# A decoder layer on one core: the opening written as one explicit list, with c spread by rounded products and VectorE in program order

## The chip, the core and the metric

The kernel is one program on one core of a Trainium2 chip. The core has five engines that run side by side and wait for each other on semaphores: TensorE (PE in the profile; its weight loads are shown as PEld), VectorE (DVE), ScalarE (ACT), GpSimd (POOL) and SyncE (SP), which here issues nearly all transfers. Sixteen DMA engines carry these from the memory outside (HBM) into the on-chip memory.

The metric is the time of one execution in microseconds (us). The kernel before takes 1697.94 us, the median of three runs (1695.81 to 1700.74).

## What is computed

A decoder layer on x of 256 rows and 2048 columns, all in float32. Its input is modulated by a condition vector c, two mixers and a feed-forward part follow. The head of it is what matters here:

```python
mod = jax.nn.silu(c) @ w_ada[l] + b_ada[l]
sh1, sc1, g1, sh2, sc2, g2 = jnp.split(mod[:, None, :], 6, axis=-1)
h = x * (1.0 + sc1) + sh1
y = token_mixer(h, w_in[l], ...)      # proj = h @ w_in, then two mixers
x = layer_norm(DEEPNORM_ALPHA * x + g1 * y, ln1_g[l], ln1_b[l])
...
```

So no element of h is known before sums over all of c, and no product with w_in can run before a piece of h.

## The kernel before

Everything is in one function, `layer`. A float32 matrix product is made of three faster ones: each operand is split in two parts of the rounded type float32r, hi (rounded, a CAST on ScalarE) and lo (the rest, a TENSOR_TENSOR on VectorE), and hi*hi, hi*lo and lo*hi are added in PSUM. For a weight this is `split_w` (L221 the cast, L222 the difference); the products are in `ws_mm` (L308 to L310), of 128x128 by 128x256 each.

**The opening** multiplies h by 24 blocks of 256 columns of w_in (`jobs`). The 2048 rows are 16 tiles of 128, and h, kept transposed as hTh and hTl (s_86 and s_87 in listings), becomes known tile by tile. For tile k two columns of the modulation are needed, the scale and the shift. Each is a load of 1 MB of w_ada into one of four ring buffers (r) and one sum on VectorE (`ada_sum`, L241: multiply by silu(c), add up, into adac). silu(c) must stand on all 128 partitions for it: `load_c` spreads the one row by four products with a row of ones, float32, and ScalarE's Silu reads them (L136, L137) into cb. Then `prep` makes 1+scale (sc1p, L444), x*(1+scale)+shift on ScalarE (L447) and its two parts (L229, L230).

The tiles are taken in five groups of 2, 3, 3, 4 and 4 (`GROUPS`, `startup`). For each group all 24 blocks are passed through: load, split, products, and the result is copied (first group, L489, ScalarE) or added to what is there (L491, VectorE). Five of the blocks stay in PSUM through all groups instead (mm_kept). While a group runs, the modulation columns of the next are summed: `ada_goal` says how many after each block, and `ada_opening` loads three ahead. From the ninth block of the last group on, each block also ticks the background lanes, which begin with the convolution of the second mixer (`gdn_pre`).

`step` puts a pair on the list `prog`: pre (the load and the split) and post (the products and what follows). `run(3)` writes the pres three steps ahead of the posts. That is the program's order; a scheduler then settles each engine's order, except where an instruction is pinned by keep_in_program_order. SyncE issues transfers in its order, and a load waits until its buffer is free (six for raw, four for hi and for lo).

Behind the opening come ps_ba (the small products of `add_ba`), the other products with h, and in the background the mixers in lanes that a tick moves on. The second mixer ends in `gdn_turn`, which transposes its result yb (L892), scales it and splits it into ybA; products with ybA follow (L308 to L310).

## Time and profile before

| | |
|---|---|
| median of three runs | 1697.94 us |
| the profiled execution | 1696.81 us |
| its span on the core | 1694.9 us |
| mean granted TensorE clock | 0.994 |
| TensorE busy | 1646.1 us (97% of the span) |
| VectorE busy | 1236.2 us (73%) |
| ScalarE busy | 839.8 us (50%) |
| DMA, mean over the span | 244 GB/s |

The page gives busy time by engine, then the span in 40 slices of 42.4 us with busy tenths (9 is 90% or more) and the clock that was granted to TensorE. A window's row gives busy us and the number of instructions (x) by engine, then the granted clock, the share of the DMA engines and GB/s. A row of the timeline gives start, duration, engine, line, operation, what is written and read, and in brackets how long the engine idled before and on whom. A group's row gives shapes, the count, busy us and mean ns of one, and the idle time before. Neighbouring instructions of one engine overlap a little, so that a duration is some 0.08 us longer on VectorE than the distance of two starts.

### The profile page before, as it was taken

The page shows a single profiled execution, that of the slowest core. Times are in us where ns is not written, and L with a number is a line of the kernel's source. Part 1 is how long each engine was busy: PE and PEld are TensorE (multiplying, and loading weights), DVE is VectorE, ACT ScalarE, POOL GpSimd, SP SyncE. Part 2 cuts the span into 40 slices and gives each one's busy share as a digit, 9 for nine tenths or more (in the row PEclk, how much of TensorE's full clock was granted, in tenths as well). Part 3 has the DMA queues.
Part 4 walks back from the last instruction along what each step waited for, and adds up shares of the span by engine and source line. Part 5 has one row for each costly group of instructions (what it writes and reads, how often), then busy time and mean ns, then how long its engine had stood idle before and what let it go on. Part 6 is the DMA issues. An engine that isn't in the chain of part 4 may idle for free.

```text
span 1694.9 us, 28166 instructions
## 1 busy us (share of the span) xinstructions
PE 1646.1 (97%) x11077; PEld 1478.7 (87%) x11077; DVE 1236.2 (73%) x1768; ACT 839.8 (50%) x1199; POOL 34.6 (2%) x60
## 2 busy tenths in 40 slices
PE   5899999999999999999999999999999999999997
PEld 4899999789989789889988898888888888888885
DVE  6899999687985678468998786666666666555454
ACT  3544445679653754464434454444444444333341
POOL 0000000001010000000000000000000000000000
PEclk9999999999999999999999999999999999999998
DMA  9999996566875578657999477777777777766651
GB/s 370 339 362 342 362 347 217 182 189 202 265 246 173 177 230 278 200 174 266 334 366 338 139 236 234 240 230 228 222 237 231 228 227 246 238 192 191 198 191 73
DMA packets 113751, 412.72 MB, mean 244 GB/s; under 512 B 13406, under 2 KB 14446, under 8 KB 108110
## 3 DMA queue, kind: packets, MB, share of 16 engines
q1 hardware_dynamic: 110178, 400.13, 70.2%
q0 software_dynamic: 3440, 10.80, 2.4%
q8 instruction: 87, 1.43, 0.3%
q14 instruction: 46, 0.37, 0.1%
HBM read 406.59 MB, written 4.28 MB: 242 GB/s over the span
## 4 chain that ended last, share of the span: by engine, by line
PE 62%; DVE 7%; DMA 4%; ACT 3%; issue 2%; POOL 0%; DVEq 0%; ACTq 0%; POOLq 0%
PE mm L315 17%; PE mm L319 9%; PE mm L356 7%; PE mm L358 7%; PE mm L357 7%; PE mm L308 4%; PE mm L309 4%; PE mm L310 3%; DVE lo L222 3%; DMA raw<-in_w_out 1%; DVE raw_a L241 1%; ACT hi L221 1%; DMA raw<-in_w_proj_gdn 1%; PE ps L756 1%; DMA UU<-ubd 0%
## 5 line engine op out<-in xcount | busy, mean ns | idle before, releaser
L222 DVE TENSOR_TENSOR lo<-raw,hi 128x1024 fp32r<-128x1024 f32 (+2 forms) x576 | 675.5, 1178 | 365.4 <-ACT hi L221 362.6
L221 ACT CAST hi<-raw 128x1024 fp32r<-128x1024 f32 (+2 forms) x576 | 583.6, 1017 | 721.5 <-PE mm L315 196.1
L308 PE MATMUL mm<-s,hi 128*128 128x256 f32 x1232 | 349.0, 284 | 16.1 <-ACT s L229 12.0
L310 PE MATMUL mm<-s,lo 128*128 128x256 f32 x1232 | 345.2, 281 | 8.1 <-DVE lo L222 7.9
L309 PE MATMUL mm<-s,hi 128*128 128x256 f32 x1232 | 345.1, 280 | 0.0
L315 PE MATMUL mm<-s,hi 128*128 128x512 f32 x1280 | 319.6, 392 | 0.0
L315 PEld LDWEIGHTS mm<-s,hi 128*128 128x128 f32 x1280 | 228.5, 188 | 39.5
L308 PEld LDWEIGHTS mm<-s,hi 128*128 128x128 f32 x1232 | 234.1, 190 | 21.3 <-ACT s L229 13.6
L310 PEld LDWEIGHTS mm<-s,lo 128*128 128x128 f32 x1232 | 234.1, 190 | 10.0 <-DVE lo L222 9.9
L309 PEld LDWEIGHTS mm<-s,hi 128*128 128x128 f32 x1232 | 234.4, 190 | 1.8 <-issue 1.4
L319 PEld LDWEIGHTS mm<-s,lo 128*128 128x128 f32 x1280 | 169.9, 188 | 13.6
L319 PE MATMUL mm<-s,lo 128*128 128x256 f32 x1280 | 171.9, 277 | 0.0
L357 PE MATMUL mm<-lo,ach 128*128 128x512 f32 x352 | 137.0, 389 | 0.0
L356 PE MATMUL mm<-hi,ach 128*128 128x512 f32 x352 | 137.0, 389 | 0.0
L358 PE MATMUL mm<-hi,acl 128*128 128x512 f32 x352 | 136.9, 389 | 0.0
L241 DVE CUSTOM_DVE_ANT_0 r<-r,cb,cols 128x2048 f32<-128x2048 f32 x40 | 93.5, 2348 | 9.2 <-ACT cb L137 9.2
L356 PE MATMUL mm<-hi,s 128*128 128x512 f32 x192 | 78.2, 407 | 0.0
L358 PEld LDWEIGHTS mm<-hi,acl 128*128 128x128 f32 x352 | 66.1, 188 | 13.8
L356 PEld LDWEIGHTS mm<-hi,ach 128*128 128x128 f32 x352 | 66.1, 188 | 13.7
L357 PEld LDWEIGHTS mm<-lo,ach 128*128 128x128 f32 x352 | 66.1, 188 | 13.5
L358 PE MATMUL mm<-hi,s 128*128 128x512 f32 x192 | 77.0, 401 | 0.0
L357 PE MATMUL mm<-lo,s 128*128 128x512 f32 x192 | 76.1, 396 | 0.0
(314 smaller groups left out, 2260.2 us busy)
## 6 DMA issues: line engine op xcount, KB each, us to landing
raw<-in_w_ffn_in SPq DMA_DIRECT2D x176, 512.0 KB, 4.3
raw<-in_w_in SPq DMA_DIRECT2D x160, 512.0 KB, 4.6
raw_a<-in_w_ada SPq DMA_DIRECT2D x112, 512.0 KB, 4.6
raw<-in_w_ffn_out SPq DMA_DIRECT2D x88, 512.0 KB, 4.1
r<-in_w_ada SPq DMA_DIRECT2D x40, 1024.0 KB, 8.1
raw<-in_w_in SPq DMA_DIRECT2D x48, 384.0 KB, 5.6
raw<-in_w_proj_gdn SPq DMA_DIRECT2D x32, 512.0 KB, 4.6
raw<-in_w_out SPq DMA_DIRECT2D x32, 512.0 KB, 6.3
```

What stands on the lines that cost most here:

```text
L221: s_.copy(hi, raw)
L222: low = v_.tensor_tensor(lo, raw, hi.bitcast(F32), op=OP.subtract)
L241: added = v_.tensor_tensor_reduce(out=raw, in0=raw, in1=cb[:, n * part:n * part + n], scale=1.0, scalar=cols[:, col:col + 1] if first else ...
L308: t_.matmul(o, hi[:, i, c], ah, start=(first and i == 0 and t == 0), stop=False)
L309: t_.matmul(o, hi[:, i, c], al, start=False, stop=False)
L310: t_.matmul(o, lo[:, i, c], ah, start=False, stop=(last and i == kn - 1 and t == 1))
L315: t_.matmul(box[t].rearrange("p (u i) -> p u i", u=2), hi[:, i, t * P:(t + 1) * P], both[k0 + i], start=(first and i == 0), stop=False)
L319: t_.matmul(box[t][:, :S], lo[:, i, t * P:(t + 1) * P], both[k0 + i][:, 0, :], start=False, stop=(last and i == kn - 1))
L356: t_.matmul(box[h], xh, hi[:, i, :], start=start, stop=False)
L357: t_.matmul(box[h], xh, lo[:, i, :], start=False, stop=False)
L358: t_.matmul(box[h], xl, hi[:, i, :], start=False, stop=stop)
L756: t_.matmul(ps[to, n, :], lhs(n), rhs(n), start=True, stop=True)
```

## The change

It rewrites the opening and leaves the layer's arithmetic as it was but for the spread of c.

- **c** is split into hi and lo parts, one row each, and spread by eight float32r products. Idle products on a zeroed tile, whose result nobody reads, stand before (8) and behind (40).
- **The order of tiles and blocks** is one list, `make_plan`. The five kept blocks and three others take tile 0 first, four blocks in one load, then tile 1; the other 16 blocks follow in pairs with both tiles. In later groups four kept blocks go first, tile by tile, in one load each, then the others.
- **Each modulation column** has a step of its own: `after` says at which step it is loaded and summed. The first two are loaded and summed in halves. `prep` handles one tile.
- **VectorE** is wrapped (`InOrder`), so that its instructions are pinned to program order until the last group.
- The last group ticks the lanes at 12 steps instead of 16.

```diff
+class InOrder:
+        def traced(*args, **kw):
+            ins = f(*args, **kw)
+            if self.on:
+                self.tc.keep_in_program_order(ins)
...
     def load_c():
-        ones = e2("ones", [1, P])
-        v_.memset(ones, 1.0)
+        rows = [wp.tile([P, 1088], F32R, tag="lo", name="crow", bufs=4)[0:1, :] for _ in range(4)]
...
+        s_.activation(adac[:, 95:96], epsc[:, 0:1], AF.Silu)
...
+        busy(8)
+        for i in range(4):
+            split(parts[0][i], parts[1][i], cb[0:1, 512 * i:512 * i + 512])
         for i in range(4):
...
-            t_.matmul(ps, ones, cb[0:1, 512 * i:512 * i + 512], start=True, stop=True)
+            for x in range(2):
+                tc.keep_in_program_order(t_.matmul(ps, ones, parts[x][i], start=(x == 0), stop=(x == 1)))
             s_.activation(cb[:, 512 * i:512 * i + 512], ps, AF.Silu)
+        busy(40)
...
+    def prep(f, direct=False):
+        v_.tensor_scalar(sc1p[:, f:f + 1], adac[:, 16 + f:17 + f], 1.0, None, op0=OP.add)
+        hf = e2("hf", [P, S])
+        if direct:
+            s_.activation(hTh[:, f, :], x_sb[:, f, :], AF.Identity, bias=adac[:, f:f + 1], scale=sc1p[:, f:f + 1])
+            v_.tensor_scalar(hf, x_sb[:, f, :], sc1p[:, f:f + 1], adac[:, f:f + 1], op0=OP.mult, op1=OP.add)
+            v_.tensor_tensor(hTl[:, f, :], hf, hTh[:, f, :].bitcast(F32), op=OP.subtract)
+            return
+        s_.activation(hf, x_sb[:, f, :], AF.Identity, bias=adac[:, f:f + 1], scale=sc1p[:, f:f + 1])
+        s_.copy(hTh[:, f, :], hf)
+        waiting.append(lambda: v_.tensor_tensor(hTl[:, f, :], hf, hTh[:, f, :].bitcast(F32), op=OP.subtract))
...
+            if at == 8:
+                v_.on = False
+                bg["pre"].append(gdn_pre(0))
+            if at >= 8:
+                tick()
...
+    def make_plan():
+        ids = [HELD + j for j in range(KEPT)] + [HELD - 3 + j for j in range(3)]
+        add(0, 1, ids[:4], True, [False] * 4)
+        add(0, 1, ids[4:], True, [False] * 4)
+        add(1, 1, ids[:4], False, [False] * 4)
+        add(1, 1, ids[5:] + ids[4:5], False, [True] * 3 + [False])
+        for u in range((HELD - 3) // 2):
+            add(0, 2, [2 * u, 2 * u + 1], True, [True, True])
+        after = {1: [2, 3]}
+        for m, n in enumerate([5,6,8,9,10,11]):
+            after.setdefault(n, []).append(4 + m)
...
+            for k in range(k0, k0 + kn):
+                add(k, 1, list(range(HELD, HELD + 4)), False, [end and k == KT - 1] * 4)
+            for at, i in enumerate([HELD + 4] + list(range(HELD))):
+                add(k0, kn, [i], False, [i < HELD or end], at if end else None)
...
+        for n, (k0, kn, ids, post) in enumerate(plan):
+            def pre(n=n, k0=k0, kn=kn, ids=ids):
...
+                    if g == 4:
+                        v_.on = False
...
+                raw = load_w(w_in, k0, kn, c0 if len(c0) > 1 else c0[0], 256 * len(c0))
+                for m in after.get(n, []):
+                    ada_load(m)
...
+                hi, lo = split_w(raw, kn, 256 * len(c0), False, 0)
+                while waiting:
+                    waiting.pop(0)()
+                for m in after.get(n, []):
+                    ada_next(m)
+                    if m % 2 and m < 2 * KT:
+                        prep(m // 2, m == 3)
```

Three places show how the instructions move. The first is VectorE's list from the start; ISA rows are the sums of `ada_sum` and the reading of their result. Before:

```order
L131 MEMSET ones 1x128
L241 ISA r_95,adac<-r_95,cb,cols 128x2048
L241 ISA adac 128x1
L241 ISA r_95,adac<-r_95,cb,cols 128x2048
L241 ISA adac 128x1
L241 ISA r_96,adac<-r_96,cb,cols 128x2048
L241 ISA adac 128x1
L241 ISA r_97,adac<-r_97,cb,cols 128x2048
L241 ISA adac 128x1
L222 TENSOR_TENSOR lo<-raw,hi 128x512
L444 TENSOR_SCALAR sc1p<-adac 128x2
```

And in the changed kernel, where all pinned rows have the line of the wrapper (L107):

```order
L107 TENSOR_TENSOR crow<-cb,crow 1x512 x4
L107 ISA r_95,ada_half<-r_95,cb,cols 128x1024
L107 ISA ada_half 128x1
L107 ISA r_95,adac<-r_95,cb,ada_half 128x1024
L107 ISA adac 128x1
L107 ISA r_95,ada_half<-r_95,cb,cols 128x1024
L107 ISA ada_half 128x1
L107 ISA r_95,adac<-r_95,cb,ada_half 128x1024
L107 ISA adac 128x1
L107 TENSOR_SCALAR sc1p<-adac 128x1
L107 TENSOR_SCALAR hf<-x_sb,sc1p,adac 128x256
L107 TENSOR_TENSOR s_87<-hf,s_86 128x256
```

Four whole sums before the first 1+scale have become four half sums of two columns. On SyncE the loads behind them moved too: before, four columns of w_ada and one load of x stood ahead of the first w_in; now these are two columns in halves, one tile of x, two loads of w_in, and then the two columns of tile 1.

The second place is ScalarE at the turn from the first group to the second: L511 copies a finished block, L477 and L478 make a tile of h, L260 casts a weight (128x768 from the second group on, but for the kept blocks). In the changed kernel:

```order
L260 CAST hi<-raw 128x1024
L511 COPY v_93<-mm 128x512 x3
L477 ACTIVATE hf<-x_sb,adac,sc1p 128x256
L260 CAST hi<-raw 128x1024
L478 CAST s_86<-hf 128x256
L260 CAST hi<-raw 128x1024 x2
L260 CAST hi<-raw 128x768 x4
```

Before, the turn read:

```order
L489 COPY qk_98<-mm 128x512
L221 CAST hi<-raw 128x512 x2
L489 COPY qk_99<-mm 128x512
L221 CAST hi<-raw 128x512 x3
L221 CAST hi<-raw 128x768 x4
```

The Identity of the third tile of the coming group (L477) now stands ahead of the coming group's first cast; before, no tile of h was made at the turn itself.

The third place is TensorE where the products with ybA begin; tp are the transposes of yb. Before:

```order
L892 MATMUL tp<-cst,yb_6630 128x128 x8
L356 MATMUL mm<-hi,s_86 128x512
L357 MATMUL mm<-lo,s_86 128x512
L358 MATMUL mm<-hi,s_87 128x512
```

and twelve products further on in the same list:

```order
L356 MATMUL mm<-hi,s_86 128x512
L357 MATMUL mm<-lo,s_86 128x512
L358 MATMUL mm<-hi,s_87 128x512
L308 MATMUL mm<-ybA,hi 128x256
L309 MATMUL mm<-ybA,hi 128x256
L310 MATMUL mm<-ybA,lo 128x256
```

And in the changed kernel:

```order
L390 MATMUL mm<-hi,s_86 128x512
L391 MATMUL mm<-lo,s_86 128x512
L392 MATMUL mm<-hi,s_87 128x512
L987 MATMUL tp<-cst,yb_6585 128x128 x8
L342 MATMUL mm<-ybA,hi 128x256 x2
L987 MATMUL tp<-cst,yb_6585 128x128 x4
L343 MATMUL mm<-ybA,hi 128x256
```

The products that stood between the transposes and the first ybA product are now ahead of both.

## The prediction

> **What bounds the kernel now.** I read the page first, then the opening (the first 303 us) in windows, its timeline, and groups of instructions.

> ```profile
> span 1694.9 us, 28166 instructions
> PE   5899999999999999999999999999999999999997
> DVE  6899999687985678468998786666666666555454
> PEclk9999999999999999999999999999999999999998
> DMA  9999996566875578657999477777777777766651
> ```

> TensorE (PE) is full in 38 of 40 slices. What it lacks lies in the first slices, and there VectorE (DVE) and the DMA engines are full too. So the opening has three resources near their limits, and work brought forward can meet any of them.

> ```profile
> core 0: us, PE busy (x) PEld busy (x) DVE busy (x) ACT busy (x) POOL busy (x), PEclk, DMA share, GB/s
> 0.00:10.00 10.00, 7.16 (x8) 2.49 (x8) 0.24 (x3) 3.42 (x5) 0.89 (x5) 1.00 0.75 235
> 10.00:20.00 10.00, 0.00 (x0) 0.00 (x0) 9.71 (x10) 1.82 (x4) 0.00 (x0) 1.00 1.02 408
> 20.00:30.00 10.00, 8.37 (x57) 8.37 (x58) 7.51 (x12) 5.80 (x12) 0.00 (x0) 1.00 1.02 422
> 30.00:40.00 10.00, 6.65 (x38) 6.04 (x38) 9.75 (x11) 3.62 (x6) 0.00 (x0) 0.77 1.03 405
> 40.00:50.00 10.00, 9.09 (x68) 8.89 (x68) 6.43 (x10) 6.21 (x12) 0.00 (x0) 0.89 0.98 364
> 50.00:60.00 10.00, 8.49 (x67) 7.68 (x67) 8.45 (x12) 8.73 (x18) 0.00 (x0) 1.00 0.78 260
> 60.00:80.00 20.00, 18.54 (x160) 18.01 (x158) 17.92 (x30) 9.68 (x14) 0.55 (x1) 1.00 0.99 372
> 80.00:120.00 40.00, 39.31 (x341) 39.15 (x342) 39.68 (x51) 17.70 (x26) 0.00 (x0) 1.00 0.93 350
> 120.00:180.00 60.00, 58.50 (x498) 57.29 (x497) 57.99 (x70) 26.56 (x35) 0.00 (x0) 1.00 0.95 359
> 200.00:300.00 100.00, 100.00 (x885) 100.00 (x884) 97.90 (x131) 51.39 (x67) 3.12 (x5) 1.00 0.81 286
> ...
> L456 PE MATMUL ps_ba<-s,wbh x32: 276/276/276, 303.2 to 308.5; 128*32 128x256 f32 x32
> ...
> 9.66 0.60 ACT L137 ACTIVATE cb<-ps_c 128x512 f32<-128x512 f32 x1 [1.11 <-PE ps_c L136]
> 10.29 2.35 DVE L241 CUSTOM_DVE_ANT_0 r<-r,cb,cols 128x2048 f32<-128x2048 f32 x1 [9.24 <-ACT cb L137]
> 12.56 2.35 DVE L241 CUSTOM_DVE_ANT_0 r<-r,cb,cols 128x2048 f32<-128x2048 f32 x1
> 18.33 1.96 ACT L221 CAST hi<-raw 128x512 fp32r<-128x512 f32 x3 [8.08 <-DMA raw<-in_w_in]
> 20.20 1.09 ACT L447 ACTIVATE hf<-x_sb,adac,sc1p 128x256 f32<-128x256 f32 x2
> 21.64 0.80 PE L308 MATMUL mm<-s,hi 128*128 128x256 f32 x2 [12.02 <-ACT s L229]
> ```

> Undisturbed, TensorE starts 885 products in 100 us, 0.113 us each. The opening has 24 blocks x 16 tiles x 6 = 2304 products, 260.4 us. They run from 21.6 to 303.1, where ps_ba follows. So 42.7 us are lost: 21.6 before the first product and 21.1 behind it. By counts, from 21.6 to 60 only 230 products run where 340 fit (12.4 us lost); from 60 to 180 there are 999 for 1062 (7.1 us); from 200 on, none is lost. The windows' edges make up the rest.

> **Term A, the first product.** Before, four modulation columns must land and be summed; now two do, in halves. The bytes ahead of the last half are 2.37 MB (c and cols 0.14, rel_bias 0.13, 2.10 of w_ada). The rows give 2.35 MB by 10 us and 0.41 MB/us after. The first block of w_in had 4.99 MB up to its end, so its bytes were through at 16.5; ScalarE got it at 18.33, 1.9 us later. With that lag the last half is there at 11.9. A half takes 1.2 (2.27 between two whole ones, 10.29 to 12.56), so the sums end at 13.1. ScalarE's Identity of tile 0 follows after 0.2 and takes 0.6 (half of L447's 1.09 for two): 13.9.

> ```profile
> L222 DVE TENSOR_TENSOR lo<-raw,hi 128x1024 fp32r<-128x1024 f32 x49 | 59.2, 1223 | 1.9 <-ACT hi L221 1.7
> L221 ACT CAST hi<-raw 128x1024 fp32r<-128x1024 f32 x49 | 51.3, 1055 | 53.7 <-PE mm L309 34.0 <-PE mm_kept L309 11.7 <-DVE adac L241 2.7
> L222 DVE TENSOR_TENSOR lo<-raw,hi 128x768 fp32r<-128x768 f32 x48 | 44.5, 954 | 0.0
> L241 DVE CUSTOM_DVE_ANT_0 r<-r,cb,cols 128x2048 f32<-128x2048 f32 x40 | 93.5, 2348 | 9.2 <-ACT cb L137 9.2
> L491 DVE TENSOR_TENSOR kq<-kq,mm 128x512 f32<-128x512 f32 x32 | 21.7, 684 | 5.2 <-PE mm L310 5.1
> L315 PE MATMUL mm<-s,hi 128*128 128x512 f32 x1280 | 319.6, 392 | 0.0
> ```

> In ScalarE's new order the weight's cast stands behind that Identity, so its 1.06 comes on top: the **first product is at 14.9**, 6.7 us earlier. The spread of c must be done when the first half lands. The quickest whole column landed 7.4 us behind its issue, which I take for the first, issued at 1.55:

> ```profile
> DMA to landing us min/median/max: 7.4/9.6/14.0
> ```

> So it was there at 9.0 and its half, by the same rate, 1.3 earlier, at 7.7. Four one-row casts end at 4.6 (0.65 each, as L221 at 18.33, from c's landing at 2.4), the differences at 5.6, the last product (L315: 0.39) at 6.1 and the last Silu near 7.1: hidden. The price of a rounded product from one row isn't in the trace. Its bounds are nothing and that of the float32 ones; since c's last Silu stood at 9.66 with those, the upper end delays the sums by at most 2.1. I take L315's, the same width and type. The 48 idle products cost nothing while they end before 14.9: 40 of them from 6.1 take 4.5 us at 0.113, or 8.5 at the slow rate of term B; the cover is thin in the second case (14.6).

> **Term B, the first two tiles.** The eight tile-0 blocks are 48 products, 5.4 us: TensorE is through at 20.3. Tile 1 needs two further columns. Another 3.3 MB stands ahead of the second (1.2 of weights and x, 2.1 of w_ada), so it lands at 20.0; VectorE sums it by 22.3, the Identity ends at 23.0: **2.7 us** idle. Ten steps of 24 products follow, 2.72 us each: 50.2 without a wait. VectorE's list from 23.4 to the last difference of group 0 holds ten differences (1.14 each with the overlap of 0.08), five sums (2.27) and 0.8 for two tiles, 23.6 us; casts that stand behind copies of finished products in ScalarE's order hold it up by some 3 us (an estimate from 0.6 a copy, five of them late), so it is through at 50.0, and TensorE at 50.9. The first cast of group 1 stands behind the Identity of tile 4 on ScalarE, and that behind the tenth sum, which runs from 50.0 to 52.3 and is followed by Identity (0.6) and cast (1.06): that ends at 53.9, **3.0 us** idle. Without that order the cast would have been ready; this is the one place where the explicit list adds a wait, and every later cast is queued behind it.

> Idle time also cools the clock. From 30 to 50 the granted clock was 0.77 and 0.89, and in the cold stretch a product took twice as long:

> ```profile
> 36.50:41.50 5.00, 5.00 (x24) 0.50 1.05 409
> ```

> 24 in 5 us, where 44 fit: 2.3 us lost. Two waits stood ahead of it, the longest of the opening after the first product:

> ```profile
> PE mm L308 <- ACT hi L221: 3.9, 5, 2.0
> PE mm L310 <- DVE lo L222: 3.8, 5, 1.4
> ```

> Each new gap is longer than either of these but shorter than both, and stands alone; I count two thirds of one cold stretch, **1.5 us**, between none and two. [...]

> **Term C, groups 1 to 4.** The loads, sums, differences and adds are the same in number. VectorE's work in group 2 by the rows: 3 x 1.22 + 20 x 0.95 for lo, 19 x 0.68 adds, 8 x 2.35 sums, 1.7 for the three tiles, less 0.08 overlap on each of 53, 52 us; TensorE's is 432 x 0.113 = 48.8. So VectorE lags 3.2 us there, the DMA engines have 17.5 MiB to bring, which at the 372 GB/s of 60 to 80 (a share of 0.99) takes the whole of it, and group 1 (six sums) is even. Before lost 7.1. Between 3.2 and 7.1 I take **6**, near the row that was measured, since a fixed VectorE order removes no work and lets one late column hold the blocks behind it.

> Sum: 14.9 + 2.7 + 3.0 + 1.5 + 6 = 28.1 lost instead of 42.7, so the last opening product is at 288.5, **14.6 us earlier**.

> **Term D, behind the opening.** The last group ticks the background lanes 12 times instead of 16, so the mixer's work stands 24 to 48 products later on TensorE. At the first ybA product it had a lead, which it loses:

> ```profile
> 753.56 1.03 PE L892 MATMUL tp<-cst,yb 128*128 128x128 f32 x8
> 760.98 0.28 PE L308 MATMUL mm<-ybA,hi 128*128 128x256 f32 x1
> L232 ACT ACTIVATE ybA<-tp,nwc x4: 677/683/686, 754.7 to 758.9; 128x512 fp32r<-128x512 f32 x4
> L233 DVE SCALAR_TENSOR_TENSOR ybA<-tp,nwc,ybA x4: 741/744/749, 756.3 to 760.3; 128x512 fp32r<-128x512 f32 x4
> ```

> Now eight transposes (1.03), a rounding (0.68) and a difference (0.74) stand bare: **2.5 us** given back. Bounds: 0 if the first products need less, 7.4 (753.56 to 760.98) if the whole turn is bare. The bare parts add to 2.5, so I stay there.

> Net 12.1 us. The profiled execution took 1696.8 (span 1694.9 and 1.9 around it), 1.1 under the median of 1697.9. So **1684.7**.

> **Rivals.**
> 1. *VectorE never waits.* Its opening work is 66 x 1.22 + 40 x 0.95 (lo), 76 x 0.68, 40 x 2.35, 10 for the tiles and 36 convolution steps:

> ```profile
> L583 DVE SCALAR_TENSOR_TENSOR cv<-kq,cols,cv 128x254 f32<-128x254 f32 x8 | 3.9, 482 | 0.0
> ```

> Less the overlap that is 269 us. From 7.7, with 3 us of early waits and 3 for the last block, the opening ends at 282.7, 20.4 earlier, 17.9 net: 1678.9. For: 97.9 of 100 busy from 200 to 300. Against: each late column now stops the list.
> 2. *The clock cools fully at both gaps.* Two stretches of 2.7 us lost instead of 1.5 in all: 1688.6. [...]
> 3. *Given back.* In the windows above VectorE idled 24.4 us, 9.8 of them in the first ten. If the other 14.6 come again in the new list, the opening ends at 294.3, 8.8 earlier, 6.3 net: 1690.5, or up to 1695.4 if the turn before ybA is bare as a whole. For: those idles came from casts that wait for landings and free buffers, and the buffers are the same. Against: tile 0 of eight blocks gives TensorE work while they fill.
> 4. *Slower: adds in strict order.* An add reads a finished product. In a fixed order it holds up the next block's difference, which TensorE then waits for. There are 76 adds. Before, adds waited 6.2 us in all, 0.08 each, where the order could be chosen:

> ```profile
> DVE kq L491 <- PE mm L310: 5.1, 8, 1.1
> DVE v L491 <- PE mm L310: 0.9, 2, 0.6
> ```

> At 0.35 each, passed on whole, 26.6 us are added: 1711. It is slower than before from 0.17 on. Against: differences run three blocks ahead of the add, some 6 us.
> 5. *The start doesn't move TensorE*, because the landings set the pace of all of group 0: about 1697.

> **How the numbers follow.** Forecast 0.54 (1680 to 1689; 0.25 of it without cooling, 1683.2), rival 1 0.15, rival 2 0.10, rival 3 0.12, rival 4 0.05, rival 5 0.04. The range 1675 to 1694 takes in rivals 1 to 3 and the bounds of c's spread (+2.1) and of term D; it leaves rivals 4 and 5 and some tails. About 0.3% (5.1 us) is what a measurement can tell from no change: below 1692.8 lie the forecast, rivals 1 and 2 and two thirds of 3, 0.87; the rest of 3 and rival 5 make 0.08; slower 0.05.

> **What would show it.** Right: first product near 14.9 behind a cast; idle TensorE near 20 to 23 and 51 to 54; the last opening product near 288; a wait of 2 to 3 us before ybA. Wrong: a first product after 17 (landings), a halved clock between 24 and 45 (cooling), more than 10 us lost from 54 to 180 with adds waiting for products (rival 4), or more than 5 us more idle behind the opening.

## The result and the profile after

The changed kernel takes 1688.72 us, the median of 6 runs (1685.69 to 1690.71), beside 1699.09 for the kernel before. The ratio is 0.9937, with a 95% interval from 0.992 to 0.9954. The profiled execution took 1687.22 us and its span is 1685.1, 9.8 us shorter than before. The forecast had been 1684.7. So the time lies in the forecast range of 1675 to 1694, and the gain is 0.6% where 0.8% was forecast.

First the head of the page of the changed kernel: span, busy tenths, clock and DMA in 40 slices, now of 42.1 us.

```profile
span 1685.1 us, 28203 instructions
PE   8999999999999999999999999999999999999997
DVE  7899999888985687568988786666666666555454
PEclk9999999999999999999999999999999999999998
DMA  9999987666775578558998477777777777765661
```

TensorE's first two slices rose from 5 and 8 tenths to 8 and 9; the others show nothing. The opening has to be read in windows, the same ones as before:

```profile
0.00:10.00 10.00, 8.62 (x29) 7.08 (x30) 4.93 (x11) 6.05 (x10) 0.89 (x5) 1.00 0.70 227
10.00:20.00 10.00, 9.05 (x69) 8.65 (x68) 9.16 (x14) 2.49 (x3) 0.00 (x0) 1.00 1.02 414
20.00:30.00 10.00, 8.01 (x64) 7.46 (x63) 9.18 (x10) 6.46 (x8) 0.00 (x0) 1.00 1.03 417
30.00:40.00 10.00, 10.00 (x87) 10.00 (x86) 7.04 (x9) 7.32 (x12) 0.00 (x0) 1.00 1.01 411
40.00:50.00 10.00, 9.03 (x75) 8.62 (x74) 9.04 (x10) 5.93 (x11) 0.00 (x0) 1.00 1.02 415
50.00:60.00 10.00, 6.82 (x53) 6.02 (x52) 7.31 (x10) 7.16 (x11) 0.00 (x0) 1.00 1.02 404
60.00:80.00 20.00, 20.00 (x179) 20.00 (x178) 19.05 (x24) 8.46 (x11) 0.00 (x0) 1.00 0.87 313
80.00:120.00 40.00, 40.00 (x344) 39.85 (x343) 39.16 (x58) 18.86 (x25) 0.55 (x1) 1.00 0.98 359
120.00:180.00 60.00, 57.86 (x493) 56.91 (x493) 58.48 (x72) 26.41 (x33) 0.00 (x0) 1.00 0.96 361
180.00:200.00 20.00, 20.00 (x179) 20.00 (x178) 19.01 (x22) 8.95 (x10) 0.00 (x0) 1.00 0.97 360
200.00:300.00 100.00, 98.84 (x864) 98.08 (x864) 95.68 (x124) 50.16 (x64) 3.11 (x5) 1.00 0.83 288
sum 300.00, PE 288.23 PEld 282.68 DVE 278.04 ACT 148.25 POOL 4.55; mean PE 26.20 PEld 25.70 DVE 25.28 ACT 13.48 POOL 0.41
```

From 20 to 50 there are 226 products where 163 stood before, and the granted clock is 1.00 throughout. From 50 to 60 there are now fewer (53 for 67): that is the turn from group 0 to group 1. From 120 to 180, 493 for 498: nothing was won there.

For a sharper account I sorted the 2304 products of the opening by their start and cut them at the groups (288, 432, 432, 576, 576 products). What a group takes beyond its count times 0.1133 us is lost:

| us | before | changed |
|---|---|---|
| first product | 21.64 | 15.00 |
| lost in group 0 | 13.29 | 7.21 |
| group 1, with the turn to it | 3.35 | 3.53 |
| group 2 | 3.89 | 4.92 |
| group 3 | 0.02 | 0.02 |
| group 4 | 0.02 | 1.73 |
| last product starts | 303.13 | 293.34 |

The start and group 0 gave 12.7 us; groups 1, 2 and 4 took 2.9 back. Behind the opening nothing changed in sum: 9.8 earlier at its end, 9.8 at the end of the span.

### The profile page after: what moved, and what is told of

The parts are those of the page before. It is cut to its first block, busy times and chain, and to the rows that moved or that the text cites. A ratio compares the mean times of both kernels' runs of the same rounds, so it can differ in the third digit from the quotient of the medians.

```text
span 1685.1 us, 28203 instructions
## 1 busy us (share of the span) xinstructions
PE 1645.2 (98%) x11125; PEld 1482.3 (88%) x11125; DVE 1240.0 (74%) x1776; ACT 842.0 (50%) x1190; POOL 34.5 (2%) x60
## 4 chain that ended last, share of the span: by engine, by line
PE 65%; DMA 5%; DVE 5%; ACT 3%; issue 2%; POOL 0%; DVEq 0%; ACTq 0%; POOLq 0%
PE mm L349 17%; PE mm L353 9%; PE mm L390 7%; PE mm L392 7%; PE mm L391 7%; PE mm L342 4%; PE mm L344 4%; PE mm L343 4%; DVE lo L107 2%; DMA raw<-in_w_proj_gdn 2%; DMA raw<-in_w_out 1%; ACT hi L260 1%; DMA UU<-ubd 1%; DVE raw_a L107 1%; PE ps L851 1%
## 5 line engine op out<-in xcount | busy, mean ns | idle before, releaser
L107 DVE TENSOR_TENSOR lo<-raw,hi 128x1024 fp32r<-128x1024 f32 (+1 forms) x562 | 675.7, 1204 | 356.8 <-ACT hi L260 354.1
L260 ACT CAST hi<-raw 128x1024 fp32r<-128x1024 f32 (+1 forms) x562 | 581.3, 1036 | 710.7 <-PE mm L349 196.0
L349 PE MATMUL mm<-s,hi 128*128 128x512 f32 x1280 | 319.6, 392 | 0.0
L107 DVE CUSTOM_DVE_ANT_0 r<-r,cb,cols 128x2048 f32<-128x2048 f32 (+1 forms) x40 | 91.8, 2296 | 2.5 <-ACT cb L175 2.4
```

The lines of the kernel that those rows point to most:

```text
L107: ins = f(*args, **kw)
L260: s_.copy(hi, raw)
L349: t_.matmul(box[t].rearrange("p (u i) -> p u i", u=2), hi[:, i, t * P:(t + 1) * P], both[k0 + i], start=(first and i == 0), stop=False)
```

## Experiments

The runs come in three series. In each, the kernel before ran beside the others on the same chip; it had medians of 1697.95, 1705.16 and 1699.3 us. The ratio to it is what compares across series. The trace of one execution shows more than the medians, whose runs of one kernel spread over some 5 us. But it is one execution, and the last section tells of two things that differ between executions of one kernel.

**c by float32 products** in the changed kernel:

```diff
-            for x in range(2):
-                tc.keep_in_program_order(t_.matmul(ps, ones, parts[x][i], start=(x == 0), stop=(x == 1)))
+            tc.keep_in_program_order(t_.matmul(ps, ones.bitcast(F32), cb[0:1, 512 * i:512 * i + 512], start=True, stop=True))
```

> The changed kernel with c spread by four float32 products as before; all else as changed. In the changed kernel's trace the first half sum starts at 7.93, behind both its load (estimated there at 7.7) and the last Silu (7.20 to 7.80). Theory A, the spread is on the path to the first product: the last Silu ends near 10.3 as before, the first half sum starts at 10.3, four halves in a row take 4.9, and the first product comes at 17.0 instead of 15.0; the last opening product is 1.5 to 2 us later. Rival: the landings set the pace, because the fourth half sum started only at 12.02 and waits of 0.1 stand between the halves: first product within 0.5 us of 15.0, end of the opening unchanged. Whole time 1688 to 1692 in either case, so the places in the trace decide.

Ratio 0.9952 [0.9934, 0.997]. The first product, in this run's timeline:

```profile
18.03 0.28 PE L339 MATMUL mm_kept<-s,hi 128*128 128x256 f32 x1
```

That is 3.0 us later than in the changed kernel, more than the 2.1 I had as the upper bound: c was on the path. But group 0 then loses 5.33 us instead of 7.21, since the waits at tile 1 take up part of it, and the opening ends 1.2 later (294.50).

**Without the idle products**:

```diff
-        busy(8)
-        busy(40)
```

> The changed kernel without the 48 idle products. Theory: TensorE meets its first products at half clock (0.213 us instead of 0.115 apart) for 3.4 us or more, as before the change; but the next thing it waits for, tile 1, comes from VectorE's sums at 22.8 whatever TensorE does, and the 48 products of tile 0 need 10.2 us at most even wholly cold, from 15.0 to 25.2. If the clock rises within 3.4 to 6 us, tile 0 ends at 22 to 23.5 and nothing or up to 0.7 us is lost at tile 1: the end of the opening moves by 0 to 1 us. Rival: the idle products carry the clock through all of group 0; without them the waits of 2 us keep it cold, as from 35.8 to 42.0 in the kernel before, and 2.5 to 5 us are lost.

Ratio 0.9974 [0.9959, 0.9988], the least gain of all. The first product stood at 15.19, but then:

```profile
15.00:18.00 3.00, 2.81 (x12) 2.69 (x13) 2.83 (x3) 1.09 (x2) 0.00 (x0) 1.00 1.00 410
58.00:61.00 3.00, 1.83 (x9) 1.83 (x10) 1.85 (x3) 3.00 (x5) 0.00 (x0) 0.75 0.64 259
```

In the first row TensorE is busy for 2.81 us and starts 12 products, where 25 fit at 0.113: they run at half rate (0.213 apart). The granted clock reads 1.00 in this row all the same; the trace's records of it begin only with its first rise, here at 18.53. The opening ends at 296.74, 3.4 later, where 0 to 1 was expected. The second row, at the turn, shows the same; it also occurs in kernels with the idle products (below), so from the trace only the start can be laid to the edit: group 0 loses 9.08 us instead of 7.21. By the median it is 4.2 us in all, by the ratios 6.

**VectorE's order left free**:

```diff
-        self.tc, self.engine, self.on = tc, engine, True
+        self.tc, self.engine, self.on = tc, engine, False
```

> The changed kernel with VectorE's opening left to the scheduler (nothing of it pinned). Theory: in groups 1 and 2 VectorE is full (58.5 of 60 us busy from 120 to 180), so its order can't matter much there; losses of 3.5 us in group 1 and 4.9 in group 2 stay within 2 us of that, and the whole opening within 2 us. Rival: the strict order is what the change lives from; without it TensorE loses 5 us or more in addition. Other rival: the strict order costs time, as adds and late columns hold the differences; without it the losses of groups 1 and 2 fall from 8.4 to under 5 us.

Ratio 0.9958 [0.9942, 0.9974]. The opening ends at 299.71, 6.4 us later in this profile, where at most 2 were expected. Group 1 loses 5.74 us instead of 3.53, but some of it is a stretch at half clock at the turn, which came in one profile of the changed kernel too (4.27 there). Groups 3 and 4 lose 2.58 and 2.88, nearly all of it in a way that is told in the last section and that came with the order fixed, too. Beside that second profile of the changed kernel, with the same two stretches at half clock, and without groups 3 and 4, about 1.5 us remain, as much as the medians differ; the intervals overlap, so that it isn't settled that the order is worth anything.

**Casts ahead of copies at the turn.** In the changed kernel ScalarE's timeline at the turn, with the first product of group 1:

```profile
53.91 0.59 ACT L511 COPY v<-mm 128x512 f32<-128x512 f32 x1 [2.29 <-PE mm L344]
54.58 0.15 DVE L107 TENSOR_SCALAR sc1p<-adac 128x1 f32<-128x1 f32 x1
55.04 0.58 ACT L511 COPY v<-mm 128x512 f32<-128x512 f32 x1 [0.55 <-PE mm L344]
55.52 0.60 ACT L477 ACTIVATE hf<-x_sb,adac,sc1p 128x256 f32<-128x256 f32 x1
56.02 1.03 ACT L260 CAST hi<-raw 128x1024 fp32r<-128x1024 f32 x1
57.11 0.38 PE L342 MATMUL mm_kept<-s,hi 128*128 128x256 f32 x1 [2.10 <-ACT hi L260]
```

The cast that TensorE waits for stands behind two copies of blocks that TensorE has only just finished, and behind the Identity. The edit pins both copies behind three casts and moves each tile's Identity into the next step (pinned there for tile 4):

```diff
+        def rest_of():
+            keep = tc.keep_in_program_order if f == 4 else (lambda ins: ins)
+            keep(s_.activation(hf, ...))
+            s_.copy(hTh[:, f, :], hf)
+            v_.tensor_tensor(hTl[:, f, :], ...)
+        waiting.append(rest_of)
...
+                    copied = s_.copy(dst, pairs_of(box[i]))
+                    if kn == 2 and i >= 14:
+                        tc.keep_in_program_order(copied)
```

> The changed kernel with one thing moved: at the turn to the second group ScalarE casts the three coming weights before it copies the last two finished blocks, and the Identity of tile 4 stands behind the first of these casts. In the changed kernel's trace TensorE stands still for 2.4 us there (54.7 to 57.1), while ScalarE copies (55.04), makes tile 4 (55.52) and casts (56.02 to 57.05), and VectorE idles 2.4 us for the same cast. Theory: the wait is ScalarE's order alone; it shrinks to 0.5 us or less and the end of the opening comes 1.5 to 2.3 us earlier. Rival 1: the difference of that block, behind the tenth sum on VectorE, is as late: the wait shrinks by under 1 us. Rival 2: the wait goes, but VectorE, full in groups 1 and 2, gives it back there: the last opening product stays within 0.7 us of 293.3.

Ratio 0.9933 [0.991, 0.9955]. The cast now runs before TensorE needs it, and group 1 follows group 0 without a gap:

```profile
52.84 1.06 ACT L260 CAST hi<-raw 128x1024 fp32r<-128x1024 f32 x1 [1.27 <-DMA raw<-in_w_in]
54.67 0.19 PEld L342 LDWEIGHTS mm_kept<-s,hi 128*128 128x128 f32 x1
54.71 0.60 ACT L480 ACTIVATE hf<-x_sb,adac,sc1p 128x256 f32<-128x256 f32 x1 [0.81 <-DVE sc1p L107]
```

The 720th product, the last of group 1, stands 1.4 us earlier than in the changed kernel. So the wait at the turn was ScalarE's order, as forecast. The Identity stood in it as I had said; the copy ahead of that, of the block that TensorE finished last, I had not counted. The edit moves both, so their shares aren't told apart. The end of the opening, expected 1.5 to 2.3 us earlier, came 2.2 later in this profile (295.54): groups 3 and 4 lost 2.58 us each, by the wider spacing of the last section. The ratio can't be told from the changed kernel's.

**What sets group 2.** Two runs tell VectorE from the transfers. In one the eight sums read 64 elements each, in the other they are whole and their loads are left out. (The sums here are whole ones of 2048 elements; only the first two columns are summed in halves.)

```diff
+            if 16 <= m < 24:
+                v_.tensor_tensor_reduce(out=raw[:, :64], in0=raw[:, :64], in1=cb[:, :64], ...)
+                continue
```

> The changed kernel, but the eight half-column sums of columns 16 to 23, which VectorE makes while TensorE works on group 2, read 64 elements instead of 1024 (a part of the modulation is left out). Theory: group 2 is set by VectorE, which is busy for 58.48 of the 60 us from 120 to 180; eight pairs of sums of about 1.2 us each go, and with them the waits of TensorE there, so that group 2 loses 0 to 1 us instead of 4.9, and the end of the opening comes 4 to 5 us earlier. Rival: the blocks of x and the weights land too late there; the waits stay, and group 2 loses 4 to 5 us as before.

```diff
-            dma.dma_start(raw[:, n * h:n * h + n], w_ada.tile(...))
+            if not 16 <= m < 24:
+                dma.dma_start(raw[:, n * h:n * h + n], src)
```

> The changed kernel without the loads of the weights of columns 16 to 23 of the modulation; the sums read what an earlier load left in their buffers (a part of the modulation is computed from other weights). Theory that VectorE sets group 2: its sums are as long as before, and group 2 loses 4 to 5 us as before, the time changes by less than 1 us. Rival, the transfers set it: 8 MB less to move in some 50 us takes the late landings away, group 2 loses 0 to 2 us, and the end of the opening comes 3 to 5 us earlier.

Windows of group 2, from 120 us to its end, in the changed kernel:

```profile
120.00:140.00 20.00, 19.09 (x161) 18.67 (x161) 19.49 (x26) 8.44 (x11) 0.00 (x0) 1.00 0.96 359
140.00:161.00 21.00, 19.76 (x166) 19.24 (x165) 20.77 (x28) 9.89 (x13) 0.00 (x0) 1.00 0.97 364
```

with short sums:

```profile
120.00:140.00 20.00, 20.00 (x179) 20.00 (x178) 16.22 (x30) 10.20 (x14) 0.00 (x0) 1.00 1.02 408
140.00:161.00 21.00, 21.00 (x187) 21.00 (x187) 19.00 (x28) 10.38 (x12) 0.00 (x0) 1.00 1.02 413
```

and without the loads:

```profile
120.00:140.00 20.00, 19.37 (x166) 19.21 (x166) 19.90 (x26) 8.51 (x12) 0.00 (x0) 1.00 0.67 193
140.00:161.00 21.00, 20.00 (x169) 19.65 (x168) 20.23 (x28) 9.62 (x13) 0.00 (x0) 1.00 0.95 341
```

The third column of a row is VectorE's busy time, the last but one the DMA share. With short sums VectorE has room, TensorE is full and group 2 loses 0.01 us instead of 4.92, though more bytes move. With nearly half of the bytes gone in the first 20 us (193 GB/s for 359), VectorE is as full as before and group 2 still loses 3.97. So VectorE sets group 2. (Of the 4.92 us, 3.0 stand in five gaps between products; the rest is the wider spacing of the last section.) The opening ends at 289.48 with short sums, 3.9 earlier, and at 298.77 without the loads, 5.4 later, since groups 0, 1, 3 and 4, which that edit leaves alone, lost 6.2 more in its profile. The ratios are 0.9901 [0.9875, 0.9927] and 0.9926 [0.9898, 0.9954].

**Sixteen ticks instead of twelve**:

```diff
-            if at == 8:
+            if at == 4:
-            if at >= 8:
+            if at >= 4:
```

> The changed kernel with the mixer's lanes advanced from the fourth column block of the last group of the opening on, as in the kernel before (16 ticks), instead of from the eighth (12 ticks). Theory, term D: the first ybA product waited 4.6 us in the changed kernel since the lanes run 24 to 48 products later; with 16 ticks it waits for less than 1 us, and from there on the run stands 3 to 5 us better than the changed kernel, if nothing wins it back later. Rival: that wait was won back elsewhere behind the opening (the changed kernel had lost 0.7 us less than before by the end), so the time stays within 1 us; and if the lanes' 4 more ticks crowd the last group, it loses 1 to 3 us there.

Ratio 0.992 [0.9897, 0.9943]. What TensorE waited for from 600 to 760 us: in the kernel before,

```profile
PE mm L310 <- DVE lo L222: 4.1, 2, 3.5
```

in the changed kernel,

```profile
PE tp_u L861 <- DMA UU<-ubd: 1.7, 1, 1.7
PE tp L987 <- DVE ybA L107: 1.0, 1, 1.0
PE mm L344 <- DVE lo L107: 0.7, 1, 0.7
PE mm L342 <- ACT ybA L271: 0.5, 1, 0.5
```

and in this run,

```profile
PE mm L344 <- DVE lo L107: 3.8, 2, 3.6
```

With 16 ticks the waits at ybA go, and the wait of 3.6 us for a lo that the 12 ticks had shrunk to 0.7 comes back. So both theories were half right: the wait at ybA is the ticks' doing (1.5 us in these rows, not the 4.6 of the expectation), and the ticks pay for it elsewhere. The wait of 1.7 us for UU, too, stands in this stretch of the changed kernel alone. In sum TensorE waits 4.1 us in it before, 3.9 in the changed kernel and 3.8 with 16 ticks. (Most of the small products of `add_ba` now ran between those of the last group, so the end of the opening isn't to be compared here.)

**Both tiles first** in group 0:

```diff
-        add(0, 1, ids[:4], True, [False] * 4)
-        add(0, 1, ids[4:], True, [False] * 4)
-        add(1, 1, ids[:4], False, [False] * 4)
-        add(1, 1, ids[5:] + ids[4:5], False, [True] * 3 + [False])
+        add(0, 2, ids[:2], True, [False] * 2)
+        add(0, 2, ids[2:4], True, [False] * 2)
+        add(0, 2, ids[4:6], True, [False, True])
+        add(0, 2, ids[6:], True, [True] * 2)
```

> The changed kernel with both tiles of the first pair ahead of the first product (group 0 in pairs of two tiles as in the other groups, four half-column pairs of sums ahead of it) instead of tile 0 of eight column blocks first. Theory: the first product starts 4 to 6 us later, near 19 to 21 us, and since the waits at tile 1 then go (2 to 4 us), the end of the opening comes 1 to 4 us later than in the changed kernel. Rival: the order of tiles in group 0 is worth all of term A, and the end comes 6 us later; or nothing, because the later sums set the end of group 0 either way, and the end stays within 1 us.

Ratio 0.992 [0.9892, 0.9947]. The first product:

```profile
20.23 0.58 PE L342 MATMUL mm_kept<-s,hi 128*128 128x256 f32 x1 [6.76 <-ACT hi L260]
```

It starts 5.2 us later, but the end of the opening only 1.5 later (294.81): behind it group 0 loses 3.69 us instead of 7.21. The early start is mostly waited away again.

The last series has the changed kernel once more, and three others.

> The changed kernel itself, once more, beside the other three. Every theory: the ratio to the kernel before is 0.992 to 0.995, as measured first. What differs between its profile and the first one (after how many of the early waits TensorE runs at half clock, and how long its products run 118 instead of 113 ns apart) is the part of the spread that no edit makes: I expect 1 to 5 us of it.

1688.94 us, ratio 0.9935 [0.9919, 0.9952]: the same. In its profile the clock was halved twice in the opening, which the first profile didn't show, and the opening ended 1.2 us later (294.54).

**The list alone**: the edits of the float32 products, the free order and both tiles first, together.

> The changed kernel with three of its parts undone together: c spread by float32 products, VectorE's order left to the scheduler, and both tiles of the first pair ahead of the first product. The explicit list, the sums in their load's step and the 12 ticks remain. Theory: each part cost 1 to 3 us when it was undone alone, and the three overlap little, so the end of the opening comes 3 to 7 us later than in the changed kernel; the other 3 to 7 of the 10 us gained are the list's own, which lets the blocks and sums of group 0 follow their loads. Rival: the parts stand in for each other; all three undone give back 8 us or more, and the list by itself is worth nothing.

1694.43 us, ratio 0.9953 [0.9936, 0.9971]. Its opening ends at 300.06, 5.5 and 6.7 us later than in the two profiles of the changed kernel, 3.1 earlier than before. By these traces the three parts hold some two thirds of what was won, and the list with its sums in step the rest. In group 0 alone the list holds more: its last product stands at 59.1 (before 67.4, changed 54.7). But the ratios, 0.9953 and 0.9935, give the three parts under a third, and the intervals overlap. The eight times fall into two clusters, three at 1688.6 to 1688.9 and five at 1694.3 to 1695.3; what parts them I could not find, and the profiled execution (1694.6) is of the slower one. So the list alone is worth something, but how the gain divides stays open. What the halved first sums and the loads of four blocks are worth was not tried alone.

**Two columns later, four columns later.** The cast edit of above, and tile 11's two columns in the first steps of group 3; the second kernel moves tile 4's columns as well:

```diff
+            late = 2 if n == 2 else 0
             for m in range(count):
+                if m >= count - late:
+                    after.setdefault(len(plan) + m - count + late, []).append(base + m)
+                    continue
-                due, x = (m + 0.5) / count * total + 0.0, 0
+                due, x = (m + 0.5) / (count - late) * total + 0.0, 0
...
-        for m, n in enumerate([5,6,8,9,10,11]):
+        for m, n in enumerate([5,6,8,9,11,12]):   (the second kernel only)
```

> The changed kernel with ScalarE's casts of group 1 ahead of the last copies of group 0 and of tile 4's Identity (as in the run that took the wait at the turn away), and with the two columns of tile 11 loaded and summed in the first two steps of group 3 instead of the last of group 2; the other six sums of group 2 are spread evenly. Theory that VectorE sets group 2 by its 52 us of work against 48.8 of products: without 4.7 us of sums it is through in time, group 2 loses 0 to 1.5 us instead of 4.9, group 3 loses 0 to 1, and with the 2 us of the turn the end of the opening comes 5 to 6 us earlier than in the changed kernel. Rival: the sums only collide later, group 3 loses what group 2 wins.

> The same, and the two columns of tile 4 are loaded and summed one and two steps later, across the end of group 0, too. Theory: the four waits of 0.7 us each of TensorE between 46 and 52 us come from VectorE's list in which a sum stands ahead of a difference; with the last sum past the end of group 0 one or two of them go, 0.5 to 1.5 us better than the kernel with two later. Rival: the waits come from landings of the weights and stay, or tile 4 is late and TensorE waits for it in group 1, 1 to 2 us worse.

With two later: 1685.78 us, ratio 0.9915 [0.9899, 0.9932]. Group 2:

```profile
120.00:140.00 20.00, 20.00 (x174) 20.00 (x173) 20.00 (x26) 9.01 (x12) 0.00 (x0) 1.00 0.91 331
140.00:160.00 20.00, 20.00 (x172) 20.00 (x172) 20.00 (x28) 6.76 (x9) 0.00 (x0) 1.00 1.00 399
```

No wait is left in it (it still loses 1.22 us; its products run a little wider apart, as the last section tells). Group 3 has one wait of 0.8. The end of the opening, expected 5 to 6 us earlier than in the changed kernel, came no earlier in this profile (293.40 for 293.34). What groups 1 and 2 won, 6.1 us, was lost again: 1.3 up to the end of group 0, with a stretch at half clock, and 4.8 in groups 3 and 4, mostly by the wider spacing. By the medians the kernel is 3.2 us faster than the changed one; the intervals overlap. With four later: 1684.59 us (1683.63 to 1687.23), ratio 0.9912 [0.9896, 0.9928], and the opening ends at 292.22. Two of the four waits of TensorE near the end of group 0 are gone, one for a cast and one for a difference, as expected, but group 1 loses 2.63 where the other lost 1.15. The two can't be told apart by time. The second is the fastest kernel of the study, 4.35 us under the changed kernel by the medians of one series; the intervals of the two ratios just overlap.

## Why the prediction was right, and where it was off

**Term A** held to 0.1 us: the first product at 15.00 for 14.9, behind a cast that stands behind tile 0's Identity.

```profile
7.20 0.60 ACT L175 ACTIVATE cb<-ps_c 128x512 f32<-128x512 f32 x1 [0.26 <-PE ps_c L174]
7.93 1.28 DVE L107 CUSTOM_DVE_ANT_0 r<-r,cb,cols 128x1024 f32<-128x1024 f32 x1 [2.36 <-ACT cb L175]
13.41 0.60 ACT L473 ACTIVATE s<-x_sb,adac,sc1p 128x256 fp32r<-128x256 f32 x1 [5.61 <-DVE sc1p L107]
15.00 0.38 PE L342 MATMUL mm_kept<-s,hi 128*128 128x256 f32 x1 [0.88 <-ACT hi L260]
```

The way to it was not the one written down. The spread of c isn't hidden: the first half sum is released by the last Silu, which ends at 7.80 (forecast 7.1), and the four half sums follow each other from 7.93 to 13.3. Landings held none of them up in this profile (with both tiles first, the first half waited for its landing until 8.43); the two estimates met by luck. And the credit was wrong in kind: I passed the 6.7 us on whole. The runs show that a first product later by 3.0 and 5.2 us ends the opening later by 1.2 and 1.5. Most of an early start is spent in waits for tile 1 and the sums.

**Term B** placed both gaps, but left out what lies between them. Measured from one start to the next: 1.97 us at 20.8 (forecast 2.7) and 2.38 at 54.7 (3.0), and no cooling in this profile (1.5). The first gap was shorter because no landing set it: VectorE ran two differences from 14.98 and both sums of tile 1 behind them without a break, up to 21.9, where a landing at 20.0 had been expected to end them at 22.3. A stretch at half clock was priced at 2.3 us here and at 2.7 in rival 2; in the runs below most lasted 3.41 us and cost some 1.5. That gaps of this length leave the clock alone, the 0.25 of the forecast at 1683.2 (1684.7 less this 1.5), no run shows: in this profile the granted clock stayed at 1.00 behind both, but nine of the thirteen profiles of the change and its variants have a stretch at half clock. Yet group 0 and the turn lost 9.5 us (7.21, and 2.27 of group 1's) where 7.2 was forecast. The step that failed is "Ten steps of 24 products follow, 2.72 us each: 50.2 without a wait". Products ran at 0.118 instead of 0.113 from 24 to 46, and four of them from 46 to 52 came 0.7 to 0.8 us behind the one before, two held up by a cast and two by a difference. Group 0's last product came at 54.73, not at 50.9, and the tenth sum ended at 54.6, not at 52.3. That casts behind copies hold VectorE up had been counted with 3 us. From 20 to 56 it was

```profile
DVE lo L107 <- ACT hi L260: 4.4, 6, 1.7
```

so this was under-sized, and its other half, TensorE waiting for the same casts and differences, was not counted at all. One such chain, on ScalarE and then VectorE:

```profile
49.60 0.59 ACT L511 COPY v<-mm 128x512 f32<-128x512 f32 x1 [1.49 <-PE mm L344]
50.08 1.05 ACT L260 CAST hi<-raw 128x1024 fp32r<-128x1024 f32 x1
51.17 1.23 DVE L107 TENSOR_TENSOR lo<-raw,hi 128x1024 fp32r<-128x1024 f32 x1 [0.33 <-ACT hi L260]
```

ScalarE waits 1.49 us for a finished product to copy it, and only then makes the cast that VectorE, and TensorE behind it, waits for. What was lost beyond the forecast, 2.3 us, is the first part of the miss.

**Term C** is the second: groups 1 to 4 lost 7.9 us without the turn, 6 was forecast. The mechanism is shown for group 2: VectorE's lag there, put at 3.2 us as the lower bound, and the runs with short sums and with two columns later took the waits away. Of the rest, 1.7 us stand in group 4, where before lost nothing: there TensorE waits once for a cast, for 1.1 us. The idle of VectorE that I hoped the list would not bring back (rival 3) did come back whole: by the windows above it idled 22.0 us of the first 300, 5.1 of them in the first ten, so 16.9 behind that. Before, it was 16.4 (the 14.6 of the prediction leaves out the window from 180 to 200). That rival's opening was to end at 294.3; it ended at 293.3, where the forecast had 288.5. Its time, 1690.5, is also nearer to the measured 1688.72 than the forecast. Its condition was nearer to the truth than mine.

**Term D** named a wait that came: TensorE waits for ybA for 1.5 us (forecast 2.5), and not at all with 16 ticks. But it was counted as a net loss, and the same delay of the lanes took 2.8 us off another wait (3.5 to 0.7). In sum nothing was given back, which by luck made up for half of what the opening missed: 4.8 us less in the opening, 2.5 more behind it, 2.3 in all (a gain of 9.8 in the span for 12.1). The rest of the distance to the median is mostly that the forecast was taken off the profiled execution before (1696.81), not off the median, and that the median now lies 1.5 above the profiled one.

Rival 4 fell: TensorE waited for an add once in the opening, for 0.7 us, and the free order is not faster. Rival 5 (the start doesn't move TensorE) fell as it was put, though most of the early start was spent.

## What to carry to other kernels

An earlier start is worth what the next limit leaves of it: undo it alone and look at the end of the stage, not at the first instruction. Where an engine is busy for 97% of a stage, compare its work with the pacing engine's stage by stage; by the traces, moving two sums across a stage's border bought 2.6 us here (3.7 in group 2, 1.1 given back in group 3, the wider spacing there not counted), the early start 1.5. In an engine's order, look for copies of just finished results that stand ahead of casts the next stage waits for (at the turn here TensorE waited 2.10 us for such a cast; with the casts ahead of copies and Identity group 1 ended 1.4 us earlier).

## What the hardware showed unexpectedly

**Two spacings at one clock.** TensorE's products, back to back and with no wait, start either 113 or 118 ns apart. The row from 200 to 300 in the run with casts ahead of copies:

```profile
200.00:300.00 100.00, 100.00 (x853) 99.77 (x852) 94.11 (x120) 50.24 (x62) 3.11 (x5) 1.00 0.81 285
```

It is as busy as the kernel before, at the same granted clock of 1.00, with 853 products for 885. Two executions of one kernel differ as well; the changed kernel from 95 to 125, in its first profile and then in its second:

```profile
95.00:125.00 30.00, 30.00 (x258) 30.00 (x257) 29.16 (x45) 14.02 (x19) 0.55 (x1) 1.00 1.01 373
95.00:125.00 30.00, 29.99 (x265) 29.82 (x264) 29.16 (x45) 13.75 (x18) 0.55 (x1) 1.00 1.02 376
```

The spacing mostly changes at a wait and then stays, in groups 3 and 4 for 130 us: 2.56 us for each 576 products. Five of the profiles (free order, casts first, without the loads, both last kernels) ran both groups at 118, the others at 113 or nearly. The profile of the fastest kernel thus has some 5 us of its opening taken by this (less what group 4's wait had cost the changed kernel). Nothing tried here decides which spacing comes.

**Half clock after short gaps.** Up to group 2 the kernels with two columns later and with casts ahead of copies are the same, but from 20 to 30 us the first starts 14 products fewer (52 for 66), a loss of 1.6 us, though the longest idle time of TensorE shortly ahead was 1.7 us in both. Such stretches, of 2 to 4 us, came between 16 and 28 us or between 57 and 65, in nine of the thirteen profiles, but not in the first one of the changed kernel. The prediction's 1.5 us is the price of one of them.

```profile
21.47:24.88 3.41, 1.52 (x8) 1.17 (x9) 3.06 (x7) 2.87 (x4) 0.00 (x0) 1.00 1.01 410
24.88:28.29 3.41, 3.41 (x18) 3.41 (x18) 3.28 (x4) 1.73 (x2) 0.00 (x0) 0.50 1.03 415
```

```profile
18.87:22.28 3.41, 2.69 (x24) 2.49 (x22) 3.41 (x3) 0.62 (x1) 0.00 (x0) 1.00 1.03 407
22.28:25.69 3.41, 2.15 (x14) 1.78 (x15) 3.04 (x7) 3.07 (x5) 0.00 (x0) 1.00 1.03 420
```

In the first kernel TensorE idles for 1.89 us of one window, and the next window is halved. In the second the border at 22.28 splits the same idle time into 0.72 and 1.26, and nothing is halved. The gap at the turn shows it again: the changed kernel's first profile has it split into 0.98 and 1.20, its second has 2.11 in one window and runs the next at half clock. Over all fourteen profiles, from the first rise to 80 us, the fifteen windows at full clock that a halved one followed had 1.67 us of idle time or more; of the others one had 1.73, all the rest 1.64 or less. About half a window of idle time, 1.67 us of 3.41, was the least ahead of a halved one in these traces. In the kernel before, TensorE idles for 2.41 us of the window from 32.00 to 35.41, with 4 products in it, and the next two windows are halved. So whether a gap of 2 us costs a stretch depended on where it fell in the grid, which no edit set. This was read off the traces afterwards; no run was made to test it, nor one with idle products that end closer to the first product.
